# Attention of a hybrid DiT block: the scores' second pass over 128 partitions, and high and low parts of the values in one stationary operand

## The chip, the cores and the metric

The kernel runs on one core of one Trainium2 chip. The metric is the time of one execution on the device in microseconds (us). TensorE multiplies matrices, VectorE (DVE in the rows), ScalarE (ACT) and GpSimd (POOL) work element by element, and SyncE (SP) starts the transfers.

## What is computed

One block of a diffusion transformer over 512 tokens and 256 context tokens with 1024 features, all in float32: a feed-forward layer, a mixer, and a second feed-forward layer. The mixer has a window attention, a gated linear recurrence (HGRN) in both directions, and a gated merge of the two. The change touches the attention alone. It has eight query heads of 64 features, which share two heads of keys and values (grouped, four query heads to each), a band of blocks of 128 tokens, the 256 context tokens as further keys, and a sink in the softmax:

```python
def window_attention(q, k, v, kc, vc, sink):
    ...
    s_band = jnp.einsum('bkgnqd,bknsd->bkgnqs', qb, kb).astype(jnp.float32) * scale
    s_band = jnp.where(valid, s_band, NEG_INF)
    s_ctx = jnp.einsum('bkgnqd,bksd->bkgnqs', qb, kc).astype(jnp.float32) * scale
    sink_b = sink.astype(jnp.float32).reshape(KVH, G)[None, :, :, None, None, None]
    p = softmax_with_sink(jnp.concatenate([s_band, s_ctx], axis=-1), sink_b).astype(v.dtype)
    o = (jnp.einsum('bkgnqs,bknsd->bkgnqd', p[..., :3 * BLOCK], vb)
         + jnp.einsum('bkgnqs,bksd->bkgnqd', p[..., 3 * BLOCK:], vc))
```

## The kernel before

Every product is made of parts. A float32 operand x is split into a high part, x rounded to the narrower type float32r, and a low part, what is left; `split` (line 64) writes the high part on ScalarE and the low part on VectorE. `mm3` (line 68) then takes three passes of TensorE into one PSUM tile: high by high (line 71), moving low by stationary high (line 72), and moving high by stationary low (line 74). Each matmul comes with a weight load of its stationary operand (PEld in the rows).

The work runs in stages: the start, the first feed-forward layer, HGRN, attention, merge, the second feed-forward layer. Inside a stage the program's order is only a starting point: the framework's planner orders each engine's instructions ahead of time by its own estimates, so TensorE's stream mixes the products of several steps. PSUM has four tiles with the tag `mm` and four with `aux`.

The attention (line 788 on) goes as follows. The keys come out of a projection as [features, tokens]: partitions 0 to 63 are head 0, 64 to 127 head 1. `put_k` (line 839) writes the high part of each key head twice, on both halves of the partitions (`kk[kv]`, 128 partitions), and the low part once, on its own half (`kl`, 64 partitions per head). The values are transposed by TensorE (line 857) and split (line 858, by the helper's lines 65 and 66) into `vh` and `vl`, each [tokens, 128], the two heads side by side. `q_pair` (line 860) makes the rotated queries of two heads; for each, `q` holds the high part on the head's half of the partitions and the low part on the other half.

`head_scores` (line 878) takes four blocks of 128 queries. For each block there are two PSUM tiles, the window (`sw`, 256 or 384 columns) and the context (`sc`, 256 columns). The first pass (line 893) multiplies the 128 partitions of `q`, high and low at once, with `kk`; the second (line 895) multiplies the 64 partitions of the high part with `kl`. VectorE then adds the mask and takes minima (lines 898 and 900), ScalarE takes the exponentials (line 902), and VectorE or ScalarE scales them (lines 912 and 914). `head_out` (line 917) transposes the probabilities of each of six key tiles (line 927), splits them into `th` and `tl` (pth and ptl in the rows), and adds three passes with `vh` and `vl` into the PSUM tile `oo` (line 932). Of the 128 rows of `oo` the 64 of the wanted head are split into `oah` and `oal` (line 933). The low part for the last 256 tokens of the values lies in a tile that the rows call `tok`.

The loop at line 945 runs the scores of a head ahead of the output of the head before, and beside them go two more query projections (line 954) and five gate projections (`early_gate`, line 799), whose matmuls are those with `hh`, `hl`, `wh` and `wl` in the rows. After the last head comes the merge (line 958 on), in which `oah` and `oal` are moving operands.

Of the kernel before, what the change touches and what calls it, by code (L numbers as in the profile page):

```python
# [37 lines left out]
def view(ap, off, dims):  # L38
    """The tile's partitions with free dimensions of one's own, from an offset in elements."""
    return AP(ap.tensor, ap.offset + off, [ap.ap[0]] + [list(d) for d in dims])  # L40
# [3 lines left out]
def kernel(ctx: ExitStack, tc: tile.TileContext, i, out):  # L44
# [16 lines left out]
    def f32(ap):  # L61
        return ap.bitcast(F32)
# [5 lines left out]
    def mm3(outs, sh, sl, start, stop):  # L68
        """outs: (psum, moving hi, moving lo); sh, sl: the stationary operand."""
        for o, mh, ml in outs:  # L70
            nc.tensor.matmul(o, lhsT=sh, rhs=mh, start=start, stop=False)  # L71
            nc.tensor.matmul(o, lhsT=sh, rhs=ml, start=False, stop=False)  # L72
        for o, mh, ml in outs:
            nc.tensor.matmul(o, lhsT=sl, rhs=mh, start=False, stop=stop)  # L74
# [18 lines left out]
    def load_w(src):  # L93
        """[KD*P, 128] -> raw [P, KD, 128]"""
        w = ct([P, KD, P], "wraw", bufs=3)
        nc.sync.dma_start(w, src.rearrange("(k p) f -> p k f", p=P))
        return w
# [19 lines left out]
    # silu of c and c_ctx; csx: their high parts and their low parts, side by side for each k  # L117
# [7 lines left out]
    # x and ctx  # L125
# [10 lines left out]
    # mcol[n, v](k): the columns A, B of block k with h = xn * A + B  # L136
# [3 lines left out]
    def make_cols(n, v, shift, scale):  # L140
        """shift and scale without their bias, [P, KD] each."""
        a = ct([P, KD], f"colA{n}{v}")
        b = ct([P, KD], f"colB{n}{v}")
        jb, js = 3 * n, 3 * n + 1
        nc.vector.tensor_tensor(out=b, in0=shift, in1=vec[:, R_B + jb * KD:R_B + (jb + 1) * KD], op=ALU.add)
        nc.vector.tensor_tensor(out=a, in0=scale, in1=vec[:, R_B + js * KD:R_B + (js + 1) * KD], op=ALU.add)
        nc.vector.scalar_tensor_tensor(out=a, in0=a, scalar=1.0, in1=vec[:, R_PRE + n * KD:R_PRE + (n + 1) * KD],
                                       op0=ALU.add, op1=ALU.mult)
        mcol[n, v] = lambda k: (a[:, k:k + 1], b[:, k:k + 1])
# [8 lines left out]
    def start_mods(qt):  # L158
        """silu(c) @ w_ada for the shift and scale of ffn1's pre-norm, a quarter of the columns of each."""
# [55 lines left out]
    def rstd(z, n, scratch):  # L215
        """(mean of z*z + eps) ** -0.5"""
        ss = ct([P, 1], "ss", bufs=8)
        if isinstance(z, (list, tuple)):
            s2 = ct([P, 2], "ss2", bufs=4)
            for q, zz in enumerate(z):  # L220
                nc.scalar.activation(scratch[:, q * 512:(q + 1) * 512], zz, AF.Square, accum_out=s2[:, q:q + 1])
            nc.vector.tensor_tensor(out=ss, in0=s2[:, 0:1], in1=s2[:, 1:2], op=ALU.add)
        else:
            nc.scalar.activation(scratch, z, AF.Square, accum_out=ss)  # L224
        r = ct([P, 1], "rs", bufs=8)
        nc.gpsimd.tensor_scalar(ss, ss, 1.0 / n, EPS, ALU.mult, ALU.add)  # L226
        nc.gpsimd.tensor_tensor(out=r, in0=ss, in1=mhalf, op=ALU.pow)  # L227
        return r
# [6 lines left out]
    def make_hT(n, hh, hl, toks, xns, pool, tag="h32"):  # L235
        """Transposed modulated norm of consecutive token tiles into hh/hl [P, KD, TA]."""
        w = len(toks) * P
        c0 = toks[0] * P
        segs = []
        nx = sum(t < NX for t in toks) * P  # L240
        if nx:
            segs.append((0, nx, 0))
        if nx < w:
            segs.append((nx, w, 1))
        for k in range(KD):
            pt = ps("aux")
            for q, xn in enumerate(xns):
                nc.tensor.transpose(pt[:, q * P:(q + 1) * P], xn[:, k * P:(k + 1) * P], ident)
            h32 = ct([P, w], tag, bufs=2, pool=pool)
            for a, b, v in segs:  # L250
                ca, cb = mcol[n, v](k)
                if k == 0:
                    nc.vector.tensor_scalar(h32[:, a:b], pt[:, a:b], ca, cb, ALU.mult, ALU.add)
                else:
                    nc.scalar.activation(h32[:, a:b], pt[:, a:b], AF.Identity, bias=cb, scale=ca)
            hi = hh[:, k, c0:c0 + w]
            nc.vector.tensor_copy(hi, h32[:, :w])
            nc.vector.tensor_tensor(out=hl[:, k, c0:c0 + w], in0=h32[:, :w], in1=f32(hi), op=ALU.subtract)
            yield

# [1 line left out]
    def proj_all(ws, hT, groups, by_k=False):  # L262
        """out^T [128 columns of w, tokens] for each w, for each group of tokens (a, b), group by group or
        row of blocks by row of blocks."""
# [15 lines left out]
    def proj(w, hT, groups, outs=None):  # L280
        """out^T [128 columns of w, tokens] for each group of tokens (a, b)."""
# [12 lines left out]
    def tick(n):  # L294
        """The next steps of the work that goes on beside the products, worth n in all."""
# [7 lines left out]
    def ffn(w_in, w_out, hT, groups, ntok, pool, pieces, yacc, last, groups0=None, pre=None, ticks=0, final_pre=None,  # L303
            order=None):
        """last(t, [psum halves], yacc or None) takes the last piece's products of token tile t."""
# [82 lines left out]
    def tok_w(c, spare=False):  # L388
        """256 columns of w, to be moved: two tiles of four rows of blocks."""
# [16 lines left out]
    def proj_tok(ws, hT, toks, take):  # L406
        """out [tokens, 256 columns] for token tiles, weights moving."""
# [8 lines left out]
    # ================ ffn1 ================  # L416
# [27 lines left out]
    with tc.manual_schedule(engines={E.Activation, E.DVE, E.Pool, E.PE}):  # L444
        mods = [start_mods(q) for q in range(NQ)]
        now = None
        for n, t in enumerate(ORDER):
            prev, now = now, start_tok(t)
            if n < 4:
                next(mods[0])           # load  # L450
            if n == 0:
                load_rows()
            next(now)                   # load
            if n < 4:
                next(mods[0])           # high part
            if prev:
                next(prev)              # transposes
            next(now)                   # mean square
            if n < 4:
                next(mods[0])           # low part, products  # L460
            if prev:
                next(prev)              # out of psum
            next(now)                   # norm
# [22 lines left out]
    with tc.tile_pool(name="f1", bufs=1, reuse_waits="tile") as f1:  # L486
# [1 line left out]
        def mod_half(j, h, vs, pool):  # L488
            """[P, 512] in psum, on every partition, for each v: half h of silu(c) @ w_ada[:, j]."""
# [59 lines left out]
        def post(t, o, n, v, w4, res):  # L549
            """tok[t] = res + gg * norm(tok[t] + products)"""  # L550
# [34 lines left out]
    # ================ mixer ================  # L585
# [9 lines left out]
    with tc.tile_pool(name="mh", bufs=1, reuse_waits="tile") as mh:  # L595
# [25 lines left out]
        def hgrn_head(n, F, q):  # L621
            # pairs of directions: F, P and Q hold (backward, forward), K (forward, backward)
# [57 lines left out]
            # scores, transposed: [s, chunk, t]  # L680
# [13 lines left out]
            # states that enter the chunks of x  # L694
# [104 lines left out]
    def early_gate():  # L799
        """A gate's columns among the attention's heads, its sigmoid later."""  # L800
# [6 lines left out]
    with tc.tile_pool(name="ma", bufs=1, reuse_waits="tile") as ma:  # L807
# [24 lines left out]
        # keys of the two kv heads: the high parts twice, on both halves of the partitions, and the low parts  # L832
# [3 lines left out]
        kl = ct([P, TA], "kl", F32R, pool=ma)  # L836
        KG = ((0, T), (T, TA))

        def put_k(a, b, z):
            for kv in range(2):  # L840
                for h in range(2):
                    nc.scalar.copy(kk[kv][H[h], a:b], z[H[kv], :b - a])
                nc.vector.tensor_tensor(out=kl[H[kv], a:b], in0=z[H[kv], :b - a], in1=f32(kk[kv][H[kv], a:b]), op=ALU.subtract)
# [4 lines left out]
        vh = ct([P, NT, P], "vh", F32R, pool=ma)  # L848
        vl_ = (ct([P, T], "vl", F32R, pool=ma), spare[:, TA:])
        vl = [vl_[t // NX][:, t % NX * P:(t % NX + 1) * P] for t in range(NT)]  # L850
        o = proj(wcols(C_AV), hT, KG)
        for g, (a, b) in enumerate(KG):
# [5 lines left out]
            split(vh[:, a // P:b // P, :].rearrange("p a b -> p (a b)"), vl_[g], pt[:, :b - a])  # L858

        def q_pair(g):  # L860
            """rotated queries of heads g and g + 4, transposed, on partitions 0-63 and 64-127."""
# [16 lines left out]
        def head_scores(g, kv, qq):  # L878
            h = kv * 4 + g
            rr = H[kv]  # L880
# [4 lines left out]
            for b in range(NX):  # L885
# [4 lines left out]
                # high and low part of q against the high part of k, then high part of q against the low part of k  # L890
# [3 lines left out]
                for o, ks in cols:  # L894
                    nc.tensor.matmul(o, lhsT=q[rr, bq], rhs=kl[rr, ks], start=False, stop=True)  # L895
# [21 lines left out]
        def head_out(g, kv, probs):  # L917
# [3 lines left out]
            for u, kt in enumerate(kts):  # L921
# [10 lines left out]
                mm3([(oo[:, cc], th[:, cc], tl[:, cc])], vh[:, kt, :], vl[kt], u == 0, u == len(kts) - 1)  # L932
            split(oah[rr, g, :], oal[rr, g, :], oo[rr, :])
# [102 lines left out]
    # ================ ffn2 ================  # L1036
# [33 lines left out]
def shape_constants():  # L1070
    """Tables that depend on shapes alone."""
# [31 lines left out]
```

## Time and profile before

| what | value |
|---|---|
| median of three runs | 1520.56 us (1520.05 to 1521.59) |
| span of the profiled execution, first to last instruction | 1516.8 us |
| around the span, against the median | 3.8 us |
| TensorE busy with matmuls | 1470.7 us, 97% of the span |
| VectorE busy | 866.2 us, 57% |
| ScalarE busy | 509.9 us, 34% |
| mean granted clock of TensorE | 0.989 |

The profile is one execution. Busy time is the union of the records on an engine, and a matmul's record lasts until its last result is written, so the records of matmuls in a row overlap: what one costs in a stream is the distance from its start to the next start. A granted clock of 1.00 is 2.4 GHz and 0.50 is 1.2 GHz.

### The profile page before, as it was taken

The page shows a single profiled execution, that of the slowest core. Times are in us where ns is not written, and L with a number is a line of the kernel's source. Part 1 is how long each engine was busy: PE and PEld are TensorE (multiplying, and loading weights), DVE is VectorE, ACT ScalarE, POOL GpSimd, SP SyncE. Part 2 cuts the span into 40 slices and gives each one's busy share as a digit, 9 for nine tenths or more (in the row PEclk, how much of TensorE's full clock was granted, in tenths as well). Part 3 has the DMA queues.
Part 4 walks back from the last instruction along what each step waited for, and adds up shares of the span by engine and source line. Part 5 has one row for each costly group of instructions (what it writes and reads, how often), then busy time and mean ns, then how long its engine had stood idle before and what let it go on. Part 6 is the DMA issues. An engine that isn't in the chain of part 4 may idle for free.

```text
span 1516.8 us, 20710 instructions
## 1 busy us (share of the span) xinstructions
PE 1470.7 (97%) x8368; PEld 1216.5 (80%) x8368; DVE 866.2 (57%) x1421; ACT 509.9 (34%) x821; POOL 57.3 (4%) x87
## 2 busy tenths in 40 slices
PE   5999999999999999999999999999999899999997
PEld 3688888888888887789888677788778788888886
DVE  6856564666654434765786757743457544434444
ACT  6532121212121122533333557632336222222221
POOL 3200000000000001200001100000000000000001
PEclk9999999999999999999999899999999999999999
DMA  9564332455551111231221111023335533233301
GB/s 305 176 189 125 111 111 78 119 165 158 162 153 43 55 42 56 79 88 40 57 58 49 56 42 43 28 78 97 93 108 175 189 96 96 88 107 97 97 29 55
DMA packets 177895, 151.45 MB, mean 100 GB/s; under 512 B 6408, under 2 KB 152328, under 8 KB 177800
## 3 DMA queue, kind: packets, MB, share of 16 engines
q1 hardware_dynamic: 177800, 150.14, 32.6%
q8 instruction: 65, 1.06, 0.3%
q14 instruction: 30, 0.25, 0.1%
HBM read 148.02 MB, written 2.10 MB: 99 GB/s over the span
## 4 chain that ended last, share of the span: by engine, by line
PE 72%; issue 15%; DVE 6%; DMA 4%; ACT 2%; POOL 1%; SPq 0%; DVEq 0%; POOLq 0%; ACTq 0%
PE mm L71 21%; PE mm L72 21%; PE mm L74 21%; DMA wa<-w_ada 3%; PE mm L895 1%; PE aux L927 1%; PE aux L72 1%; PE aux L71 1%; PE mm L893 1%; PE aux L74 1%; POOL rs L227 1%; DVE macc L498 1%; DVE wl L66 1%; DVE wa0l L178 1%; ACT w L224 1%
## 5 line engine op out<-in xcount | busy, mean ns | idle before, releaser
L71 PE MATMUL mm<-hh,wh 128*128 128x512 f32 (+1 forms) x1440 | 513.5, 357 | 0.2 <-ACT sg L333 0.2
L72 PE MATMUL mm<-hl,wh 128*128 128x512 f32 (+1 forms) x1440 | 492.4, 355 | 0.0
L74 PE MATMUL mm<-hh,wl 128*128 128x512 f32 (+1 forms) x1440 | 449.6, 357 | 0.3 <-DVE wl L66 0.3
L71 PEld LDWEIGHTS mm<-hh,wh 128*128 128x128 f32 x1440 | 271.2, 188 | 59.1 <-issue 0.9
L72 PEld LDWEIGHTS mm<-hl,wh 128*128 128x128 f32 x1440 | 271.3, 188 | 40.9 <-DVE hl L426 0.6
L65 ACT CAST wh<-wraw 128x1024 fp32r<-128x1024 f32 (+1 forms) x139 | 142.5, 1026 | 470.9 <-PE mm L72 302.9
L66 DVE TENSOR_TENSOR wl<-wraw,wh 128x1024 fp32r<-128x1024 f32 (+1 forms) x139 | 165.5, 1191 | 231.5 <-ACT wh L65 227.4
L74 PEld LDWEIGHTS mm<-hh,wl 128*128 128x128 f32 x1440 | 244.4, 189 | 22.4 <-DVE wl L66 0.5
L71 PE MATMUL mm<-woh,acth 128*128 128x512 f32 x420 | 164.3, 391 | 1.9 <-DVE am L335 1.2
L72 PE MATMUL mm<-wol,acth 128*128 128x512 f32 x420 | 164.0, 391 | 0.0
L498 DVE SCALAR_TENSOR_TENSOR macc<-wa,cs,macc 128x512 f32<-128x512 f32 x140 | 101.7, 748 | 61.8 <-DMA wa<-w_ada 60.9
L74 PE MATMUL mm<-woh,actl 128*128 128x512 f32 x420 | 130.7, 390 | 0.0
L335 DVE TENSOR_TENSOR am<-sg,mm 128x512 f32<-128x512 f32 x66 | 37.4, 594 | 116.3 <-PE mm L74 116.3
L65 ACT CAST woh<-w 128x1024 fp32r<-128x1024 f32 x42 | 44.3, 1054 | 168.3 <-PE mm L74 164.0
L71 PEld LDWEIGHTS mm<-woh,acth 128*128 128x128 f32 x420 | 78.8, 188 | 19.8 <-DVE am L335 1.6
L74 PEld LDWEIGHTS mm<-woh,actl 128*128 128x128 f32 x420 | 78.8, 188 | 16.6
L72 PEld LDWEIGHTS mm<-wol,acth 128*128 128x128 f32 x420 | 78.9, 188 | 15.9
L365 DVE TENSOR_TENSOR tok<-tok,mm 128x512 f32<-128x512 f32 x96 | 61.5, 681 | 51.3 <-PE mm L74 51.3
L66 DVE TENSOR_TENSOR wol<-w,woh 128x1024 fp32r<-128x1024 f32 x42 | 51.1, 1221 | 15.9 <-ACT woh L65 14.7
L226 POOL TENSOR_SCALAR ss<-ss 128x1 f32<-128x1 f32 x30 | 9.5, 317 | 983.7 <-ACT am L224 549.0
L65 ACT CAST acth<-am 128x512 fp32r<-128x512 f32 x66 | 34.1, 548 | 22.5 <-DVE am L335 22.2
L66 DVE TENSOR_TENSOR actl<-am,acth 128x512 fp32r<-128x512 f32 x66 | 37.5, 594 | 0.7 <-ACT acth L65 0.7
(287 smaller groups left out, 1714.4 us busy)
## 6 DMA issues: line engine op xcount, KB each, us to landing
wraw<-ffn_w_in SPq DMA_DIRECT2D x88, 512.0 KB, 4.0
wa<-w_ada SPq DMA_DIRECT2D x128, 256.0 KB, 3.2
w<-ffn_w_out SPq DMA_DIRECT2D x44, 512.0 KB, 4.5
wraw<-mix_w_in SPq DMA_DIRECT2D x42, 512.0 KB, 3.7
tok<-w_ada SPq DMA_DIRECT2D x16, 256.0 KB, 5.6
wraw<-w_out SPq DMA_DIRECT2D x8, 512.0 KB, 4.3
tok<-x SPq DMA_DIRECT2D x4, 512.0 KB, 7.6
wraw<-x SPq DMA_DIRECT2D x4, 512.0 KB, 3.2
```

The source lines that it names most:

```text
L65: nc.scalar.copy(hi, src)
L66: nc.vector.tensor_tensor(out=lo, in0=src, in1=f32(hi), op=ALU.subtract)
L71: nc.tensor.matmul(o, lhsT=sh, rhs=mh, start=start, stop=False)
L72: nc.tensor.matmul(o, lhsT=sh, rhs=ml, start=False, stop=False)
L74: nc.tensor.matmul(o, lhsT=sl, rhs=mh, start=False, stop=stop)
L178: eng.tensor_tensor(out=wl, in0=w, in1=f32(wh), op=ALU.subtract)
L224: nc.scalar.activation(scratch, z, AF.Square, accum_out=ss)
L227: nc.gpsimd.tensor_tensor(out=r, in0=ss, in1=mhalf, op=ALU.pow)
L335: nc.vector.tensor_tensor(out=m[:, :b - a], in0=s[:, :b - a], in1=up, op=ALU.mult)
L365: nc.vector.tensor_tensor(out=y, in0=y, in1=o[h], op=ALU.add)
L498: nc.vector.scalar_tensor_tensor(out=a, in0=w, scalar=cs[:, v, k:k + 1], in1=a, op0=ALU.mult, op1=ALU.add)
L893: nc.tensor.matmul(o, lhsT=q[:, bq], rhs=kk[kv][:, ks], start=True, stop=False)
```

## The change

The low part of the keys gets one tile per key head, with the same 64 rows on both halves of the partitions; ScalarE copies them to the other half. The second pass of the scores then takes all 128 partitions of `q`, so it also adds the product of the two low parts. The values get one tile `vs` in which, for each key tile and head, 64 columns of high parts stand beside 64 columns of low parts. With it as the stationary operand two passes, `th` and `tl`, give the high parts' sums in rows 0 to 63 of `oo` and the low parts' in rows 64 to 127. Behind the last pass ScalarE copies the lower half out (`ov`), VectorE adds the two halves, and the result is split from SBUF in place of PSUM. The two splits of the values become four, one for each head. A parameter of the program's construction, the size of a scratch area, is set to 1024.

```diff
-        kl = ct([P, TA], "kl", F32R, pool=ma)
+        kl = [ct([P, TA], f"kl{kv}", F32R, pool=ma) for kv in range(2)]
...
-                nc.vector.tensor_tensor(out=kl[H[kv], a:b], in0=z[H[kv], :b - a], in1=f32(kk[kv][H[kv], a:b]), op=ALU.subtract)
+                nc.vector.tensor_tensor(out=kl[kv][H[kv], a:b], in0=z[H[kv], :b - a], in1=f32(kk[kv][H[kv], a:b]), op=ALU.subtract)
+                nc.scalar.copy(kl[kv][H[1 - kv], a:b], f32(kl[kv][H[kv], a:b]))
...
-        vh = ct([P, NT, P], "vh", F32R, pool=ma)
-        vl_ = (ct([P, T], "vl", F32R, pool=ma), spare[:, TA:])
-        vl = [vl_[t // NX][:, t % NX * P:(t % NX + 1) * P] for t in range(NT)]
+        vs = ct([P, NT, 2, 2, 64], "vs", F32R, pool=ma)
...
-            split(vh[:, a // P:b // P, :].rearrange("p a b -> p (a b)"), vl_[g], pt[:, :b - a])
+            vv = vs[:, a // P:b // P]
+            src = pt[:, :b - a].rearrange("p (t v d) -> p t v d", v=2, d=64)
+            for kv in range(2):
+                split(vv[:, :, kv, 0, :], vv[:, :, kv, 1, :], src[:, :, kv, :])
...
-                    nc.tensor.matmul(o, lhsT=q[rr, bq], rhs=kl[rr, ks], start=False, stop=True)
+                    nc.tensor.matmul(o, lhsT=q[:, bq], rhs=kl[kv][:, ks], start=False, stop=True)
...
-                mm3([(oo[:, cc], th[:, cc], tl[:, cc])], vh[:, kt, :], vl[kt], u == 0, u == len(kts) - 1)
-            split(oah[rr, g, :], oal[rr, g, :], oo[rr, :])
+                vk = vs[:, kt, kv].rearrange("p a b -> p (a b)")
+                nc.tensor.matmul(oo[:, cc], lhsT=vk, rhs=th[:, cc], start=u == 0, stop=False)
+                nc.tensor.matmul(oo[:, cc], lhsT=vk, rhs=tl[:, cc], start=False, stop=u == len(kts) - 1)
+
+            ov = ct([P, T], "ov", bufs=2, pool=ma)
+            nc.scalar.copy(ov[H[0], :], oo[H[1], :])
+            nc.vector.tensor_tensor(out=ov[rr, :], in0=oo[H[0], :], in1=ov[H[0], :], op=ALU.add)
+            split(oah[rr, g, :], oal[rr, g, :], ov[rr, :])
...
-    nc = bacc.Bacc("TRN2", target_bir_lowering=False, num_devices=1)
+    nc = bacc.Bacc("TRN2", target_bir_lowering=False, num_devices=1, dynamic_dma_scratch_size=1024)
```

## Rows read from the trace of the kernel before

**Rows 1.** Page, part 1: engine, busy us, share of the span, instructions.

```profile
PE 1470.7 (97%) x8368; PEld 1216.5 (80%) x8368; DVE 866.2 (57%) x1421; ACT 509.9 (34%) x821; POOL 57.3 (4%) x87
```

**Rows 2.** Busy us by stretch: length, engines in turn, granted clock, DMA share, GB/s.

```profile
854.00:876.00 22.00, 19.21 (x44) 11.35 (x45) 15.83 (x47) 11.24 (x22) 1.26 (x1) 0.62 0.08 24
876.00:990.00 114.00, 112.81 (x564) 86.14 (x563) 78.90 (x207) 76.71 (x151) 2.57 (x2) 1.00 0.13 38
895.00:915.00 20.00, 18.88 (x90) 13.35 (x88) 15.88 (x47) 14.55 (x26) 0.00 (x0) 1.00 0.07 19
935.00:955.00 20.00, 20.00 (x106) 15.34 (x105) 14.50 (x40) 17.05 (x32) 0.00 (x0) 1.00 0.10 28
```

**Rows 3.** Timeline of matmuls at full clock: start us, length us, instruction.

```profile
896.83 0.40 PE L74 MATMUL mm<-hh,wl 128*128 128x512 f32 x1
897.06 0.40 PE L71 MATMUL mm<-hh,wh 128*128 128x512 f32 x1
...
898.16 0.28 PE L893 MATMUL mm<-tok,qq 128*128 128x256 f32 x1
898.37 0.38 PE L895 MATMUL mm<-kl,qq 64*128 64x256 f32 x1
898.69 0.51 PE L74 MATMUL mm<-hh,wl 128*128 128x512 f32 x1
899.03 0.28 PE L893 MATMUL mm<-tok,qq 128*128 128x256 f32 x1
```

**Rows 4.** Timeline of weight loads in the same stretch, with idle time before them.

```profile
897.06 0.19 PEld L893 LDWEIGHTS mm<-tok,qq 128*128 128x128 f32 x1
...
898.37 0.18 PEld L895 LDWEIGHTS mm<-kl,qq 64*128 64x128 f32 x1 [0.26 <-issue]
```

**Rows 5.** Timeline of matmuls: first second pass, low clock, last second pass.

```profile
855.09 0.50 PE L895 MATMUL mm<-kl,qq 64*128 64x256 f32 x2
...
864.05 0.58 PE L893 MATMUL mm<-kk,qq 128*128 128x256 f32 x1
...
865.07 0.69 PE L893 MATMUL mm<-kk,qq 128*128 128x384 f32 x1
...
974.05 0.38 PE L895 MATMUL mm<-kl,qq 64*128 64x256 f32 x1
```

**Rows 6.** Third pass with the values, by tile: count, ns min/median/max, forms.

```profile
L74 PE MATMUL aux<-pth,vl x32: 276/310/341, 879.0 to 987.9; 128*128 128x256 f32 x16, 128*128 128x384 f32 x16
L74 PE MATMUL aux<-pth,tok x16: 388/396/398, 877.7 to 988.8; 128*128 128x512 f32 x16
```

**Rows 7.** Timeline of passes with the values near the last head's end.

```profile
987.82 0.28 PE L72 MATMUL aux<-ptl,vh 128*128 128x256 f32 x1
987.94 0.28 PE L74 MATMUL aux<-pth,vl 128*128 128x256 f32 x1
```

**Rows 8.** Groups of VectorE and ScalarE, 854 to 990 us: busy us, mean ns | idle before.

```profile
L66 DVE TENSOR_TENSOR ptl<-aux,pth 128x512 fp32r<-128x512 f32 (+2 forms) x48 | 25.5, 550 | 10.0 <-ACT pth L65 9.8
L66 DVE TENSOR_TENSOR oal<-aux,oah 64x512 fp32r<-64x512 f32 x8 | 5.5, 686 | 4.5 <-ACT oah L65 4.4
...
L65 ACT CAST oah<-aux 64x512 fp32r<-64x512 f32 x8 | 4.6, 580 | 8.5 <-PE aux L74 8.5
```

**Rows 9.** Waits, 854 to 990 us: who for whom, us in total, times, longest.

```profile
ACT pth L65 <- PE aux L927: 22.3, 18, 5.3
...
DVE s L898 <- PE mm L895: 6.2, 9, 1.4
```

**Rows 10.** Busy us in 2 us stretches about the low clock; columns as in rows 2.

```profile
858.00:860.00 2.00, 0.89 (x3) 0.44 (x3) 2.00 (x4) 0.18 (x1) 0.84 (x1) 0.84 0.86 249
...
876.00:878.00 2.00, 2.00 (x12) 1.61 (x11) 0.94 (x5) 2.00 (x8) 0.00 (x0) 0.90 0.00 0
```

**Rows 11.** Timeline of ScalarE before the scores, as keys and values are prepared.

```profile
839.85 1.25 ACT L842 CAST kk<-s 64x512 fp32r<-64x512 f32 x2
...
848.16 0.62 ACT L65 CAST wh<-wraw 128x512 fp32r<-128x512 f32 x1 [3.29 <-issue]
```

More of the change, by code (lines that the diff above doesn't have):

```diff
@@ L879, in head_scores @@
             h = kv * 4 + g
-            rr = H[kv]
             q = qq[kv]
```

## The prediction

> **What bounds the kernel now.** I read the page's busy times first: TensorE has matmuls on 97% of the span, VectorE is busy for 57% [rows 1]. So time goes only where TensorE gets less to do, and only as far as another engine can keep up there. Next come the busy times by stretch. The attention's scores and outputs run from 854 to 990 us; I cut that at 876, where the clock is back [rows 2]. In the first 22 us the mean granted clock is 0.62 and VectorE is busy for 15.8 us. In the 114 us after it TensorE is busy for 112.8 us, VectorE for 78.9 (69%), ScalarE for 76.7 (67%). TensorE sets the pace in this longer stretch, but two engines are not far behind. Whether TensorE works or stalls inside its busy time, only the timeline of matmuls tells, by distances from start to start.
>
> **What the second pass costs.** At full clock, matmuls over 128 partitions follow each other in 0.23 us with 512 columns [rows 3] and in 0.12 us with 256 [rows 7]. Around a second pass they don't. From one first pass at 898.16 to the next at 899.03 there lie a first pass of 256 columns, a second of 256 and a gate's matmul of 512 [rows 3]: 0.87 us for what would take 0.12 + 0.12 + 0.23 = 0.47. The 0.40 us over it is the price of one trip to 64 partitions and back. The loads show how it comes about: a load of 128 partitions starts together with the matmul before its own (897.06, its matmul at 897.30), while the load of line 895 starts at 898.37, the very start of its matmul, after 0.26 us in which the load path waits for nothing that the profile names [rows 4]. The 64-row load is not brought forward behind a 128-row matmul, and the load after it isn't either.
>
> In the timeline of the stage I count 56 runs of second passes, the first at 855.09 and the last at 974.05 [rows 5] (64 matmuls, 8 of them right behind another): 11 at the low clock, 45 at the full one. At the low clock a trip with twice 256 columns takes 865.07 - 864.05 = 1.02 us [rows 5]; at half speed two such matmuls would need 4 x 0.116 = 0.46, with 0.116 as half of the 0.23 us above. That is 0.56 us a trip. In all TensorE gets back 45 x 0.40 = 18.0 us and 11 x 0.56 = 6.2 us. The columns stay, so nothing is added: a matmul of 256 columns takes 0.38 us in its record with 64 rows, and 0.28 with 128 rows [rows 3].
>
> **What the values' third pass costs.** 48 matmuls go, 16 each of 512, 384 and 256 columns [rows 6]. At 0.23, 0.174 (between its neighbours, by columns) and 0.116 us [rows 3, 7] that is 16 x 0.52 = 8.3 us, all but a little of it at full clock. TensorE is thus relieved of 18.0 + 8.3 = 26.3 us in the long stretch and of 6.2 in the first: 32.5 us.
>
> **What is added.** For each head ScalarE copies 64 x 512 out of PSUM and VectorE adds 64 x 512. The nearest rows are the present cast into `oah`, 0.58 us, and subtraction into `oal`, 0.69 us [rows 8], also from PSUM: 8 x 0.58 = 4.6 us and 8 x 0.69 = 5.5 us. The split that follows has the same shapes as now, from SBUF. Behind the ScalarE copy, which waits for the last pass, the next head's casts `pth` are queued; behind the VectorE sum, which waits for that copy, the subtractions `ptl`. Between ends of zero (the planner puts other work in front) and the waits that the present split has there, 8.5 and 4.5 us [rows 8], this may cost either engine as much again. I take no term of its own for it; it is part of the share that I choose below. `oo` is held as long as now, by one instruction of each engine. Only the last head's output is awaited soon, by the merge, 0.58 + 0.69 = 1.3 us later than now; gate matmuls of the merge cover it, and without them it costs these 1.3 us.
>
> In preparation ScalarE gets four copies of the low keys: two like the 0.62 us of the 512-column `kk` casts [rows 11], two of half the size and at most that, so 1.9 to 2.5 us. The four splits of the values handle as many elements as the two now, with two instructions more on each engine, at most 0.58 and 0.69 us each. ScalarE sits idle for 3.3 us behind them [rows 11] while TensorE runs query projections, so I cost both at nothing; with that cover gone, 3.7 us. No DMA changes, so no queue of SP or POOL is passed. The scratch area I cost at nothing: no step changes with it; its ends are below the 0.2% that a measurement here can tell from no change.
>
> **What is late next.** VectorE in the long stretch gets 78.9 + 5.5 = 84.4 us. If TensorE kept the pace the stretch would be 114 - 26.3 = 87.7 us, and VectorE would have to be busy for 96% of it. That is too much for queues in a fixed order in which VectorE waits for ScalarE (9.8 us before `ptl` [rows 8]) and ScalarE for transposes (22.3 us [rows 9]). The other end is what VectorE has done where TensorE set the pace: at most 15.88 of 20 us, 79% [rows 2]; then the stretch takes 84.4 / 0.79 = 106.8 us. I choose 87%, midway, as neither end is nearer: 97.0 us, a gain of 17.0. ScalarE would be at (76.7 + 4.6) / 97.0 = 84%, which it has reached before, 17.05 of 20 us [rows 2]. In the first stretch VectorE's idle time, 22.0 - 15.8 = 6.2 us [rows 2], is the most that can go, and part of it was waiting for line 895 [rows 9]. Between nothing and 6.2 I take the middle, 3.1. The sum is 20.1 us: the profiled span goes from 1516.8 to 1496.7, and with the 3.8 us around it the median from 1520.6 to 1500.5 us.
>
> **The rivals.** (A) TensorE keeps the pace everywhere, because the planner fills its gaps with projections of the merge: the whole 32.5 us go, 1488.1 us. For it: the merge is almost all TensorE. Against it: 96% of VectorE.
>
> (B) The engines behind stay at the 79% that the trace has: 114 - 106.8 = 7.2 us, with 3.1 before it 10.3, 1510.3 us. The chain of four instructions at each head's end speaks for it.
>
> (C) The 0.40 us is not the switch of rows, or the load stays bare over 128 rows too. Then only the third pass goes, 8.3 us: 1512.3 us. Against it: loads over 128 rows do start a matmul ahead [rows 4]. The Trainium skill, TensorE: Matmul & The Clock Gate, Part 3 (The mechanism), says that a weight load overlaps a running matmul only where their row groups differ. By that rule every load of the changed second pass would lie bare, which speaks against the change; the trace disagrees, with 0.23 us from start to start at 128 rows on both sides.
>
> (D) Slower than before, by the clock. Between 858 and 860 us TensorE was busy for 0.89 of 2 us, waiting for VectorE, and the clock fell; it was back between 876 and 878 [rows 10]. Such a stretch of 16.5 us at half clock costs up to 8.2 us. If VectorE's pace makes a gap like that in later heads too, the gain of 20.1 is gone with the third such stretch; with one in every second head, four more, it is 1500.5 + 33 = 1533.5 us. Against it: from 876 on gate and query matmuls lie between the scores. The same page, Part 1 (A second HAM failure mode: psum-queue depth-cycling), tells of a kernel whose short pauses between groups of matmuls made the clock swing; no stretch after 876 us shows it yet.
>
> **How the numbers follow.** The forecast has a chance of 0.56, A 0.15, B 0.17, C 0.05, D 0.07. Of B, 0.04 is a head's end so long that all is lost: no change within 0.2%. So faster by over 0.2% is 0.56 + 0.15 + 0.13 + 0.05 = 0.89, within it 0.04, slower 0.07. The range is 1489 to 1511 us: it leaves out D, half of C, the upper part of B and the lower end of A, about 0.2.
>
> **What would show it.** The loads of the second pass start one matmul ahead, without idle time before them, and passes of 256 columns follow in 0.12 us; 8320 matmuls; the attention's stretch about 20 us shorter; VectorE at 85 to 90% of the long stretch; waits of TensorE for VectorE where there are hardly any now; the low clock once. Wrong would be: distances of 0.2 us at the second pass (C), VectorE still under 80% with TensorE full (A, or a new stall), or a second fall of the clock (D).

## The result and the profile after

| what | before | after |
|---|---|---|
| median of four runs | 1520.30 us | 1498.61 us |
| span of the profiled execution | 1516.8 us | 1497.1 us |
| TensorE busy | 1470.7 us | 1445.2 us |

The ratio is 0.9867, with a 95% interval from 0.9852 to 0.9881: about 20 us less (the two medians lie 21.7 us apart). The forecast was 1500.5 us in a range from 1489 to 1511, so it was right. Its sum was 20.1 us, and the span fell by 19.7. The parts of the sum were less right than the sum, and most of the experiments below are about them.

The page, part 1, of the kernel after (engine, busy us, share of the span, instructions):

```profile
PE 1445.2 (97%) x8320; PEld 1204.6 (80%) x8320; DVE 870.3 (58%) x1431; ACT 515.9 (34%) x835; POOL 58.3 (4%) x87
```

There are 48 matmuls fewer, and TensorE is still busy for 97% of a shorter span, as in [rows 1]. (The end of a matmul's record is modelled, not observed.) Next the busy times by stretch (length, then PE, PEld, DVE, ACT, POOL busy, granted clock, DMA share, GB/s): after, from the first score to the clock's return, from there to the end of the last head's output, and the merge to its last product with that output:

```profile
857.00:873.50 16.50, 12.40 (x43) 9.64 (x44) 14.88 (x46) 10.23 (x21) 1.27 (x1) 0.59 0.11 32
873.50:975.50 102.00, 98.20 (x539) 79.89 (x537) 84.05 (x216) 81.32 (x160) 2.58 (x2) 1.00 0.15 42
975.50:1067.00 91.50, 91.50 (x400) 74.77 (x399) 36.52 (x44) 28.89 (x37) 0.00 (x0) 1.00 0.31 92
```

Before, the first two stretches were 22.0 and 114.0 us [rows 2]. The merge has no row there; this is it, before, from 990.5 us:

```profile
990.50:1087.00 96.50, 96.50 (x422) 78.88 (x421) 37.68 (x45) 29.12 (x37) 0.00 (x0) 1.00 0.30 88
```

So the gain has three places: 5 us in the first stretch (the first score starts at 854.65, so it was 21.4 us), 12.5 in the long one (114.5 us when it ends at 990.5, as the merge here begins), and 4.6 in the merge: from the end of the last head's output to the start of the last product with `oah` it is 96.1 us before and 91.5 after. (The windows above are cut to half microseconds.) The merge itself is the same work. It is shorter because 20 of its matmuls, of 0.23 us each, were ordered into the attention. VectorE is busy for 82% of the long stretch, TensorE for 96%.

The pattern that the prediction is about, after, in the timeline of matmuls at full clock (start us, length us):

```profile
893.86 0.29 PE L895 MATMUL mm<-tok,qq 128*128 128x256 f32 x1
893.99 0.28 PE L897 MATMUL mm<-kl,qq 128*128 128x256 f32 x1
894.11 0.40 PE L74 MATMUL mm<-hh,wl 128*128 128x512 f32 x1
894.34 0.28 PE L895 MATMUL mm<-tok,qq 128*128 128x256 f32 x1
```

Line 895 is now the first pass and line 897 the second. From one first pass to the next with the same three matmuls it is 0.48 us, where [rows 3] had 0.87. And the weight loads of the second pass and of the matmul behind it:

```profile
893.87 0.19 PEld L897 LDWEIGHTS mm<-kl,qq 128*128 128x128 f32 x1
893.99 0.19 PEld L74 LDWEIGHTS mm<-hh,wl 128*128 128x128 f32 x1
```

Each starts with the matmul ahead of its own, without the idle 0.26 us of [rows 4].

In the preparation something went against the prediction. The timeline of ScalarE, after:

```profile
841.54 0.62 ACT L844 CAST kl<-kl 64x512 fp32r<-64x512 f32 x1
842.17 0.62 ACT L842 CAST kk<-s 64x512 fp32r<-64x512 f32 x1
842.82 0.41 ACT L844 CAST kl<-kl 64x256 fp32r<-64x256 f32 x1
843.55 0.62 ACT L844 CAST kl<-kl 64x512 fp32r<-64x512 f32 x1 [0.33 <-DVE kl L843]
844.19 1.04 ACT L65 CAST wh<-wraw 128x1024 fp32r<-128x1024 f32 x1
845.26 0.86 ACT L854 COPY s<-mm 128x512 f32<-128x512 f32 x2
```

And TensorE's transposes of the values, which wait for the last of these:

```profile
845.90 0.87 PE L857 MATMUL aux<-ident,s 128*128 128x128 f32 x6 [1.53 <-ACT s L854]
```

The copies of the low keys (line 844) stand ahead of the copy of the values out of PSUM (line 854), and TensorE idles for 1.53 us. From the recurrence's last transpose to the first score it is 30.49 us (826.77 to 857.27 in the timelines); before it was 28.93 (825.72 to 854.65).

To compare runs I use a sum that leaves out the unchanged stages: from the recurrence's last transpose to the last product with `oah` in the merge. It is 260.9 us before and 240.3 after: 20.6 less. What lies outside it is the same code in all kernels here, but in their profiles it varies by itself: 824.8 to 827.0 us ahead of it, 428.3 to 433.4 behind it. That is why a difference of 1 or 2 us can show in this sum and not in the medians. Every profile is one execution; two executions of the changed kernel gave 240.33 and 240.35, but the kernel before and the same with another scratch area gave 260.9 and 261.8.

One thing differs between the runs that only one edit aimed at: how long the granted clock stays at half speed after the first scores. It is 17.1 us before and with the values alone, 13.7 in both executions of the change and with the copies on GpSimd, 6.8 in the run with a gate first, and 10.2 in the other runs below that change the kernel's steps. In the run with the scratch area it is 17.1 us, and the clock falls once more at 913 us, for 3.4 us; its sum is the longer one. At half clock 512 columns took 0.42 us before (875.62 to 876.04), at full clock 0.23. By the columns in the timelines this cost 5.1 us before, 4.9 with the values alone, 4.8 in the change and 3.5 to 4.0 in the runs with 10.2 us (an estimate). So about 1 us of a difference between two sums can be the clock's; whether the edits cause it, no run shows.

### The profile page after: what moved, and what is told of

The parts are those of the page before. It is cut to its first block, busy times and chain, and to the rows that moved or that the text cites. A ratio compares the mean times of both kernels' runs of the same rounds, so it can differ in the third digit from the quotient of the medians.

```text
span 1497.1 us, 20626 instructions
## 1 busy us (share of the span) xinstructions
PE 1445.2 (97%) x8320; PEld 1204.6 (80%) x8320; DVE 870.3 (58%) x1431; ACT 515.9 (34%) x835; POOL 58.3 (4%) x87
## 4 chain that ended last, share of the span: by engine, by line
PE 71%; issue 15%; DVE 6%; ACT 3%; DMA 2%; POOL 2%; SPq 0%; DVEq 0%; POOLq 0%; ACTq 0%
PE mm L71 22%; PE mm L72 22%; PE mm L74 22%; DMA wa<-w_ada 1%; POOL rs L227 1%; PE aux L929 1%; DVE wl L66 1%; DVE wa0l L178 1%; ACT w L224 1%; POOL ss L226 1%; ACT wh L65 0%; PE aux L935 0%; PE aux L507 0%; PE aux L936 0%; DMA tok<-ctx 0%
```

## The experiments

### The scores alone

The change without its part on the values: `vh`, `vl`, three passes, split of `oo` straight into `oah` and `oal`.

```diff
-                vk = vs[:, kt, kv].rearrange("p a b -> p (a b)")
...
+                mm3([(oo[:, cc], th[:, cc], tl[:, cc])], vh[:, kt, :], vl[kt], u == 0, u == len(kts) - 1)
+            split(oah[rr, g, :], oal[rr, g, :], oo[rr, :])
```

> The scores' second pass over 128 partitions alone; the values keep their three passes and the present split at a head's end. Theory (a trip to 64 rows and back costs TensorE 0.40 us at full clock and 0.56 us at half clock; part comes back as waits): of 24.2 us freed the trace of the change gave back 13.8 us net in the stage, less 1.5 us for ScalarE's copies of the low keys in the preparation: about 12 us less than before, ratio 0.992, and 128-row loads one matmul ahead. Rival (the gain of the whole change is mostly the values' third pass, and freed trips come back as waits for VectorE): under 6 us less, ratio above 0.996.

Measured: 1501.21 us beside 1519.40 before, ratio 0.9881 (0.9861 to 0.9900), 18 us less. That is more than either theory expected. The sum without the unchanged stages is 244.2 us, 16.8 less than before: 1.6 more in the preparation, 18.3 less in the attention. The busy times from the first score to the end of the last head's output, and of the merge:

```profile
856.50:974.10 117.60, 111.44 (x609) 92.93 (x609) 93.34 (x252) 86.80 (x171) 3.87 (x3) 0.96 0.14 41
974.10:1070.20 96.10, 96.10 (x420) 78.58 (x419) 37.31 (x44) 29.11 (x37) 0.00 (x0) 1.00 0.30 88
```

The attention is as short as with the whole change (118.3 us), with all 48 third passes still in it, and the merge as long as before. So the rival falls: the scores carry most of the gain. (Of the 16.8 us some 1.6 are the shorter half clock.) My expectation was low because I had taken the net of the whole change, in which waits had already eaten a part, for that of the scores alone.

### The values alone

The kernel before with the values' part of the change: `vs`, two passes, the sum of the halves.

```diff
-                mm3([(oo[:, cc], th[:, cc], tl[:, cc])], vh[:, kt, :], vl[kt], u == 0, u == len(kts) - 1)
-            split(oah[rr, g, :], oal[rr, g, :], oo[rr, :])
+                nc.tensor.matmul(oo[:, cc], lhsT=vk, rhs=th[:, cc], start=u == 0, stop=False)
+                nc.tensor.matmul(oo[:, cc], lhsT=vk, rhs=tl[:, cc], start=False, stop=u == len(kts) - 1)
...
```

> Two passes with the values alone; the scores keep the second pass over 64 partitions and the low keys their single copy. Theory (TensorE sets the pace, the sum of the halves is hidden): 8.3 us of matmuls go, and as trips still leave TensorE busy nearly all of it shows: 6 to 8 us less than before, ratio 0.995 to 0.996; with e1 the sum is about the whole change's 20 us. Rival (the four instructions at a head's end set the pace): under 3 us less, ratio above 0.998.

Measured: 1511.74 us, ratio 0.9952 (0.9933 to 0.9970), by the ratio 7.3 us less, as the theory had it; the sum is 254.1 us, 6.8 less than before. Its rows for the same two stretches:

```profile
855.00:988.70 133.70, 130.44 (x581) 93.72 (x581) 100.01 (x261) 91.81 (x179) 3.83 (x3) 0.94 0.12 36
988.70:1080.20 91.50, 91.50 (x401) 74.86 (x400) 36.58 (x43) 28.90 (x37) 0.00 (x0) 1.00 0.31 92
```

Of these 6.8 us two thirds, 4.6, come out in the merge: with fewer passes of the values, 20 of its matmuls were ordered ahead. The two parts alone make 16.8 + 6.8 = 23.6 us, together 20.6. They overlap by 3 us.

### 96 and 64 rows

The second pass of the first key head's four heads over the first 96 partitions, or 64; the other four heads stay at 128. With 96 rows half of the products of low by low parts are left out for these heads, with 64 all of them.

```diff
-                    nc.tensor.matmul(o, lhsT=q[:, bq], rhs=kl[kv][:, ks], start=False, stop=True)
+                    m = slice(0, 96) if kv == 0 else slice(0, P)
+                    nc.tensor.matmul(o, lhsT=q[m, bq], rhs=kl[kv][m, ks], start=False, stop=True)
```

> The change, with the second pass of the four heads of the first key head over 96 partitions in place of 128; it leaves out half of the products of low parts by low parts there. Theory (the 0.40 us comes with the form of 64 rows, whose loads are not brought forward next to loads of the whole array; 96 rows need the whole array's form): from one start to the next 0.12 us with 256 columns around the 96-row passes, loads one matmul ahead, time as the change, within 4 us. Rival (any change of the number of rows between matmuls costs it): about 28 of 56 trips come back, 28 x 0.40 = 11 us more in TensorE's stream, idle loads before half of the second passes.

> As the run with 96 rows, with 64 rows in their place: the second pass of the first key head's four heads is that of the kernel before. Theory (the form of 64 rows costs TensorE 0.40 us a trip at full clock, 0.56 at half clock): about 28 trips come back, 11 to 12 us of TensorE, of which three quarters show, as 18 of 24 us did in the run with the scores alone: 8 to 9 us more than the change, and starts at 0.2 to 0.3 us around those passes alone. Rival (the price lies in switching between key heads or PSUM tiles): no difference from the run with 96 rows.

With 96 rows the one execution took 1498.83 us, with a sum of 239.3 us: the change's 240.3, within the 1 us that the clock alone can make. Its timeline:

```profile
891.28 0.28 PE L895 MATMUL mm<-tok,qq 128*128 128x256 f32 x1
891.40 0.28 PE L898 MATMUL mm<-kl,qq 96*128 96x256 f32 x1
891.51 0.40 PE L74 MATMUL mm<-hh,wl 128*128 128x512 f32 x1
891.76 0.28 PE L895 MATMUL mm<-tok,qq 128*128 128x256 f32 x1
```

The timeline with 64 rows, at the same place in the order, for the first key head and then the second:

```profile
891.11 0.28 PE L895 MATMUL mm<-tok,qq 128*128 128x256 f32 x1
891.32 0.38 PE L898 MATMUL mm<-kl,qq 64*128 64x256 f32 x1
891.64 0.51 PE L72 MATMUL mm<-hl,wh 128*128 128x512 f32 x1
891.98 0.28 PE L895 MATMUL mm<-tok,qq 128*128 128x256 f32 x1
...
893.71 0.28 PE L895 MATMUL mm<-kk,qq 128*128 128x256 f32 x1
893.83 0.28 PE L898 MATMUL mm<-kl,qq 128*128 128x256 f32 x1
893.95 0.40 PE L72 MATMUL mm<-hl,wh 128*128 128x512 f32 x1
```

With 96 rows one first pass follows another after 0.48 us, with 64 after 0.87. It is the form of 64 rows that costs, not another number of rows, and not a change of key head or PSUM tile. The price is one of the trip: where two passes of 64 rows stand in a row, the second adds little more than its columns (rows in the last section). The Trainium skill, TensorEngine Tiling (Array Packing), Key Properties, says that a change between the array's tiling modes drains it; these rows agree, with 0.39 us for a trip at full clock. The mode itself stands in no row; passes of 96 rows behave as those of 128.

The end time was a miss. The run with 64 rows took 1501.29 us, ratio 0.9876 (0.9860 to 0.9893), beside 1498.52 of the change measured with it, 0.9851 (0.9836 to 0.9865): about 3 us, where I expected 8 to 9. Its sum is 243.7 us, 3.4 more than the change. The values-alone run is the other end of this line: with its preparation evened out (1.5 us) it has all its trips, 59, and a sum of 255.6. From 59 trips to 28 saves 12 us, 0.39 a trip; from 28 to none saves 3.4 us, 0.12 a trip. The clock favours the run with 64 rows in both steps (10.2 us at half clock beside 17.1 and 13.7). Evened out for it, as estimated above, the steps are about 10.6 and 4.5 us, 0.34 and 0.16 a trip. By their prices the 31 trips of the first step, 8 of them at half clock, cost 13.7 us, and the 28 of the second, 3 at half clock, 11.7. So the first half of the trips is paid back to three quarters or more, the second to 0.3 or 0.4 of its price. The other order, with the first key head's trips gone and the second's left, was not run.

### The sum of the halves, left out and done twice

Left out: the upper half alone is split, so the products with the low parts of the values are missing from the output. Done twice: the first sum goes into a tile that nothing reads.

```diff
-            ov = ct([P, T], "ov", bufs=2, pool=ma)
-            nc.scalar.copy(ov[H[0], :], oo[H[1], :])
-            nc.vector.tensor_tensor(out=ov[rr, :], in0=oo[H[0], :], in1=ov[H[0], :], op=ALU.add)
-            split(oah[rr, g, :], oal[rr, g, :], ov[rr, :])
+            split(oah[rr, g, :], oal[rr, g, :], oo[H[0], :])
```

```diff
+            o2 = ct([P, T], "o2", bufs=1, pool=ma)
+            nc.vector.tensor_tensor(out=o2[rr, :], in0=oo[H[0], :], in1=ov[H[0], :], op=ALU.add)
             nc.vector.tensor_tensor(out=ov[rr, :], in0=oo[H[0], :], in1=ov[H[0], :], op=ALU.add)
```

> The change without ScalarE's copy of the lower half of the output and VectorE's sum: the upper half alone is split, so the output lacks the products with the low parts of the values. 4.7 us of ScalarE and 5.5 us of VectorE go. Theory (TensorE is full again in the long stretch, 96%, since products of the merge fill its gaps): at most 2 us less than the change. Rival (VectorE sets the pace in the stage, as the prediction's share of 87% has it): 4 to 6 us less.

> The change with VectorE's sum at each head's end done twice, the first into a tile that nothing reads: 5.5 us more of VectorE. Theory (after the run without the sum, which gained nothing): TensorE is full in the long stretch and VectorE at 82%, so at most 2 us more than the change. Rival (VectorE sets the pace): 4 to 6 us more.

Without the sum: 1500.47 us, ratio 0.9872 (0.9849 to 0.9895), nothing gained. Its attention and merge:

```profile
856.70:971.50 114.80, 106.25 (x565) 86.07 (x565) 93.69 (x253) 85.85 (x171) 3.84 (x3) 0.96 0.14 42
971.50:1066.70 95.20, 95.20 (x417) 77.88 (x416) 36.77 (x43) 29.10 (x37) 0.00 (x0) 1.00 0.30 89
```

The attention is 3.5 us shorter than the change's, and the merge 3.7 us longer: 16 of its matmuls weren't ordered ahead. The sum, 240.5 us, is that of the change, with the clock 1 us in its favour. Taking 5.5 us from VectorE and 4.7 from ScalarE brings nothing, so the rival, VectorE's pace, falls as a statement on the whole stage.

With the sum twice: 1502.94 us, ratio 0.9879 (0.9864 to 0.9893), 4.4 us more than the change beside it; the trace's sum shows 2.1 of them (242.4 us):

```profile
856.10:976.60 120.50, 110.78 (x581) 89.27 (x582) 103.51 (x269) 91.14 (x179) 3.86 (x3) 0.96 0.14 40
```

Of 5.5 us more on VectorE two fifths show in the trace, three fifths if the shorter half clock is evened out, and more in the median. But TensorE doesn't wait longer for VectorE: 6.5 us in all, where it was 6.7. The trace puts 1.7 of the 2.1 us down to one place, behind the rotation of a pair of queries:

```profile
919.03 1.26 ACT L876 CAST qq<-s 64x512 fp32r<-64x512 f32 x2 [1.89 <-DVE s L829]
922.56 0.50 PE L71 MATMUL mm<-hh,wh 128*128 128x512 f32 x1 [1.89 <-ACT gg L794]
```

The sum that nothing reads stands on VectorE ahead of the rotation's last addition (line 829). ScalarE's cast of the queries waits 1.89 us for that (0.68 in the change), ScalarE's copy of a gate's projection (line 794) comes behind it, and TensorE waits 1.89 us for this copy (0.19 in the change; its own order differs there too). So the rival is right that work added on VectorE costs, but what the trace shows is its place in a chain through ScalarE, and not VectorE's share of the stretch.

### The change once more

> The change again, as the measure for the two runs beside it: 1498 to 1500 us, ratio 0.985 to 0.988.

1498.52 us, ratio 0.9851 (0.9836 to 0.9865), and the sum of 240.35 us. Its attention, for the rows above:

```profile
857.50:975.80 118.30, 110.74 (x581) 89.72 (x581) 98.73 (x261) 91.26 (x179) 3.84 (x3) 0.94 0.14 41
```

### The copies of the low keys

Later in the program, behind the values, as two copies; then on GpSimd at their old place.

```diff
+        for kv in range(2):
+            nc.scalar.copy(kl[kv][H[1 - kv], :], f32(kl[kv][H[kv], :]))
+
         def q_pair(g):
```

```diff
-                nc.scalar.copy(kl[kv][H[1 - kv], a:b], f32(kl[kv][H[kv], a:b]))
+                nc.gpsimd.tensor_copy(kl[kv][H[1 - kv], a:b], f32(kl[kv][H[kv], a:b]))
```

> The change, with ScalarE's copies of the low keys placed behind the preparation of the values, as two copies of 768 columns. Theory (these copies stand on ScalarE before the copy of the values that TensorE's transposes wait for, 1.53 us of idle TensorE at 845.9 us): that wait goes and the first score starts 1.5 us earlier after the recurrence's end; 1.5 us less than the change, about 1497 us. Rival (the first score waits for something else, the rotation of the queries): no difference, 1498.6 us.

> The change with the four copies of the low keys on GpSimd in place of ScalarE. The planner had left the later copies of the run before ahead of the copy of the values, so the wait of TensorE for it stood (1.2 us). Theory: GpSimd is idle there, the wait falls to 0.4 us or less as before the change, the first score comes 29.0 us after the recurrence's last transpose (30.5 in the change), and the time is 1.5 us below the change. Rival (the rotation of the queries holds the first score back): it still comes after 30.2 us or more.

The first took 1496.83 us, ratio 0.9851 (0.9833 to 0.9868), which looks like the 1.5 us expected, but the trace says otherwise. The planner put the two copies ahead of the copy of the values all the same; TensorE waits there and the first score comes after 30.20 us:

```profile
844.06 0.87 PE L856 MATMUL aux<-ident,s 128*128 128x128 f32 x6 [1.23 <-ACT s L853]
```

The sum is 239.7 us, 0.6 less, which the shorter half clock alone would make. The median's fall is not shown to be the edit's. With the copies on GpSimd no wait is listed:

```profile
843.12 0.40 PE L74 MATMUL mm<-hh,wl 128*128 128x512 f32 x1
843.52 0.87 PE L857 MATMUL aux<-ident,s 128*128 128x128 f32 x6
```

The first score comes after 28.96 us, as before the change. So the cause is shown: ScalarE's order in the preparation costs 1.5 us. But the median is 1498.46 us, ratio 0.9870 (0.9855 to 0.9884), no better than the change: the sum is 239.1, only 1.2 less, and the unchanged stage behind it happened to be 1.6 us longer in the profiled execution.

### A gate projection first

One of the five gate projections beside the first heads, with the copies on GpSimd.

```diff
-                if 2 * g + kv in (1, 3, 4, 5, 6):
+                if 2 * g + kv in (0, 1, 3, 4, 5):
```

> As the run with the copies on GpSimd, with one of the five early gate projections moved from the seventh place among the heads to the first, beside the first two heads' scores. Theory (in that stretch TensorE idles for 4.1 of 16.5 us, and the clock falls there): the gate's 5.5 us of matmuls fill the idle time and the clock falls later or for a shorter time; 3 to 6 us less than the run with the copies on GpSimd. Rival (that stretch is VectorE's, which gets the gate's subtraction as well, and the late heads lack filler): no difference, or up to 3 us more.

1499.05 us, ratio 0.9873 (0.9853 to 0.9894): no difference from the run with the copies on GpSimd. The clock did come back sooner. Busy us and granted clock (the last but two) without the edit, and with it:

```profile
868.00:870.00 2.00, 2.00 (x8) 1.52 (x7) 1.88 (x8) 0.51 (x2) 0.00 (x0) 0.50 0.00 0
870.00:872.00 2.00, 2.00 (x9) 1.47 (x8) 0.68 (x3) 1.24 (x3) 0.00 (x0) 0.76 0.00 0
```

```profile
864.00:866.00 2.00, 2.00 (x7) 1.53 (x6) 1.42 (x5) 1.00 (x3) 0.00 (x0) 0.51 0.00 0
866.00:868.00 2.00, 2.00 (x10) 1.68 (x9) 1.59 (x4) 0.73 (x1) 0.00 (x0) 1.00 0.00 0
```

It came back 5 us sooner, after 6.8 us at half clock in place of 13.7. By the columns this should give 2.0 us (the same kind of estimate as above); the attention takes 117.7 us in place of 118.7. The first score comes 0.5 us later and the merge is 0.7 us longer, so that the sum is 239.4 us beside 239.1. The half clock isn't all that this stretch is made of. VectorE, busy in the change for 14.9 of its 16.5 us, is the likelier bound, as the rival had it, but no run takes work of VectorE out of this stretch to show it.

### The scratch area alone

```diff
-    nc = bacc.Bacc("TRN2", target_bir_lowering=False, num_devices=1)
+    nc = bacc.Bacc("TRN2", target_bir_lowering=False, num_devices=1, dynamic_dma_scratch_size=1024)
```

> The kernel before with the scratch area's size set to 1024 and nothing else. Theory (no step uses it): ratio 0.998 to 1.002. Rival (part of the gain, or of a hidden loss, is due to it): a ratio outside 0.998 to 1.002 by more than its interval.

1519.91 us, ratio 1.0006 (0.9995 to 1.0017): it costs and brings nothing.

## Why the prediction was right, step by step

**The price of a trip, 0.40 us: right.** The pattern of three matmuls went from 0.87 to 0.48 us; 96 and 64 rows show that the form of 64 rows is the cause. The rule that rival C names from the Trainium skill, TensorE: Matmul & The Clock Gate, Part 3 (The mechanism), that a load overlaps only with matmuls of other row groups, was rightly set aside for 128 rows: the loads of line 897 start a matmul ahead.

**The values' third pass, 8.3 us: right.** Alone it showed 6.8 us in the sum, and 7.3 by the ratio of the times.

**The sum of the halves: durations right, weight wrong.** ScalarE's copy took 0.58 us and VectorE's sum 0.68. I made VectorE's 5.5 us the reason for what is late next; without them nothing was gained.

**The preparation at nothing: wrong by 1.6 us.** The cover that I named was ScalarE's idle time behind the values. The copies were ordered ahead of them, onto a step that TensorE waits for. The price of lost cover that I gave was 3.7 us, so the wrong step was the place, not the size.

**What is late next: the step that failed.** I let VectorE stretch the long part to 97.0 us at a share of 87% and gave TensorE idle time in it. It took 102.0 us with VectorE at 82%, and TensorE was full at 96%: its gaps were filled with products of the merge, as rival A said, and the merge is 4.6 us shorter. Long part and merge together fell by 17.1 us, and the term was 17.0. But the term was for the long part alone, and that gave 12.5, midway between the forecast and the 7.2 of rival B, at a share nearer to B's 79% than to mine. So the size was right by luck: VectorE's share was too high, and the merge, which the sum left out, made up for it. The first stretch, put at the middle of 0 to 6.2 us, gave 5. These 2 us more and the 1.6 lost in the preparation nearly cancel; the rest is 1.1 us by which the unchanged stages ahead came later in this profile.

Why not all of rival A's 32.5 us? TensorE's waits, after (who for whom, us in total, times, longest):

```profile
PE mm L895 <- DVE s L902: 2.3, 3, 0.9
PE mm L895 <- DVE nms L900: 2.2, 3, 1.3
PE mm L895 <- DVE qq L877: 0.9, 1, 0.9
PE aux L935 <- ACT pth L65: 0.9, 2, 0.8
PE aux L929 <- DVE ov L940: 0.7, 1, 0.7
PE aux L936 <- DVE ptl L66: 0.6, 2, 0.4
...
```

Before, TensorE waited in this stage for VectorE alone, 4.1 us in four waits. Now it waits for 8.2 us in all. These 4.1 us more and the 1.6 of the preparation are 5.7 of the 11.9 us by which the 20.6 fall short of 32.5. No single wait makes the rest. Nearly all of it lies in small pieces: outside the trips and the listed waits, 101 distances from start to start are longer by 0.06 to 0.32 us than their columns need at the granted clock, 11.0 us together, where before there were 49 with 4.9 us (an estimate from the timelines, with 0.232 us for 512 columns). What each of them waits for, the profile doesn't list. The runs show the course: the first half of the trips is mostly paid back, the second to about a third. That TensorE has by then caught up with the engines that feed it is the likely reason; it is argued, not shown. Neither the sum of the halves nor the clock nor the gate's place is the bound by itself.

Rivals B and C gave 1510.3 and 1512.3 us. Of B the share came nearly true (82%, not 79) and not the time; C's mechanism doesn't appear. For D the clock fell once, from 859 to 873 us, and not again.

## What to carry to other kernels

Matmuls over 64 partitions between others over 128 cost far more than their columns: 0.40 us a trip at full clock here. If the spare rows can be filled with something harmless or useful, do so. Read such a price from start-to-start distances in the timeline, since busy time hides it, and don't count on getting all of it back: here half of the trips gave 12 us, the other half 3.4. A step that is put on an idle engine is free only at the place where a planner puts it: look for who waits for what stands behind it.

## What the runs showed of the hardware

The price at full clock is one of the trip, and not of each matmul of 64 rows. Before, two first passes and two second passes in the timeline (x2 is two matmuls):

```profile
890.12 0.41 PE L893 MATMUL mm<-tok,qq 128*128 128x256 f32 x2
890.45 0.50 PE L895 MATMUL mm<-kl,qq 64*128 64x256 f32 x2
890.88 0.66 PE L927 MATMUL aux<-ident,s 128*128 128x128 f32 x4
```

The two of 64 rows take 0.43 us to the next start; a single one takes 0.32 (898.37 to 898.69 in [rows 3]). So the second adds 0.11 us, about what 256 columns take over 128 rows. And GpSimd copied 64 x 512 to the other half of the partitions in 0.61 us (the profile's spans on GpSimd are rough), as fast as ScalarE with 0.62:

```profile
840.28 0.61 POOL L844 CAST kl<-kl 64x512 fp32r<-64x512 f32 x1 [0.60 <-DVE kl L843]
```
